# Half of a shift vector's products moved from the gated-delta stage into the gap between output and up projection

## The chip, the cores and the metric

The kernel runs on one core of a Trainium2 chip. The metric is the device time of one execution in microseconds (us); lower is better. TensorE's instructions stand as PE (matmul) and PEld (weight load), VectorE as DVE, ScalarE as ACT, GpSimd as POOL; SP is the queue from which nearly all transfers are issued, in order.

## The reference, cut to what matters

One layer with adaptive modulation, on 128 context and 256 latent tokens of width 2048, all in float32:

```
mod = SiLU(cond) @ w_ada + b_ada          # cond: two vectors; w_ada: 2048 x 12288
shift1, scale1, gate1, shift2, scale2, gate2 = split(mod, 6)
h = RMSNorm(x)*(1+scale1)+shift1
out = mixer(h) @ w_out                    # gated DeltaNet heads and mLSTM heads; w_out 2048 x 2048
x += gate1 * RMSNorm(out)
h = RMSNorm(x)*(1+scale2)+shift2
x += gate2 * RMSNorm(relu(h @ w1)^2 @ w2) # w1 2048 x 8192, w2 8192 x 2048
```

The modulation reads 100 MB of `w_ada` for two rows of result. shift2, scale2 and gate2 (sections 3, 4 and 5 of `mod`, 2048 columns each) are not needed before the second norm, so the kernel computes them beside other work.

## The kernel before

A large product is split: each weight chunk of 2x128 rows (`raw`, 512 KB) is cast to a high part `whi` by ACT and a low part `wlo` by DVE (`wchunk`), and each product is three matmuls (high with low, high with high, low with high). `raw` has three buffers, `whi` and `wlo` two each. `gemm` goes over 8 such chunks for 512 columns of result; with `room`, the last chunks are held in buffers of their own and multiplied row group by row group at the end, so that the first row group is finished early.

The stages that matter here, in order: the last quarters of the gated-delta scan, a chain of small products, with the products of the gate projection between (`ag_block` 0 and 1: `ps_g` from `h`); the transposes of the mixer's output into `yT` (`ps_yT`); the output projection, four `gemm` calls of 512 columns (`mid`), whose weights are `w_out`; then a gap in which DVE adds the residual `x1` (`x<-x,r1r,xr`), the norm factors r1 and r2 of each of the three token tiles are computed (DVE `r1v`, `r20v` to `r22v`, POOL `r1r`, `r20r` to `r22r`), and TensorE transposes the normed tokens (`ps_hT`, with a diagonal matrix `diag` of the factors for the first four of 16 columns of tiles); then the up and down projections of `ffn`.

Modulation work is a list of generators, `S.todo`. `ada_steps` does half a section, 1024 columns, on TensorE: 8 steps of two loads of 512 KB (`raw_ada`) and 8 products of 128x32 with 256 columns, four beside each other in the array (line 206). `ada_vec` does a quarter, 512 columns, on DVE: 8 loads of 512 KB (`raw_av`) and 32 multiply-adds into `adav` (lines 234 and 236). `raw_ada` and `raw_av` share the two buffers of tag `rawa`. After each chunk of a `gemm`, `fill` adds `S.rate` to a credit and runs that many steps; `drain` runs the list down to a given number. A scheduler then orders the instructions of each engine by its own estimates, so that the rows of an engine are not those of the program, but within an engine they run strictly in that order.

In the output projection the chunks are taken as 4, 5, 6, 7, 0, 1, 2, 3; the fourth call holds the last four. The buffers of `yT` for chunks 4 to 7 have the tags `h00` and `h01`, those for chunks 0 to 3 `h10` and `h11`; the activations `hT` of the up projection take these tags over.

Of the kernel before, what the change touches and what calls it, by code (L numbers as in the profile page):

```python
# [12 lines left out]
F32 = mybir.dt.float32  # L13
# [8 lines left out]
P = 128  # L22
D = 2048
NK = D // P
# [10 lines left out]
R1, R2, R3, ND2 = 1.3, 0.9, 0.3, 1  # L35
# [8 lines left out]

def setup(S):
    nc, tc, A = S.nc, S.tc, S.A
    cp, tp = S.cp, S.tp
    c = S.c = SimpleNamespace()

# [167 lines left out]
        ada_mod(S, sec, c0 // P, m, s)  # L217


def ada_vec(S, sec, c0):  # L220

    nc, c = S.nc, S.c
    while S.av is None:
        yield 1
    acc = S.av.tile([P, 2, 512], F32, tag="adav", name="adav", bufs=1)
    for kt in range(NK):
        if kt % 2 == 0:
            raw = S.wp.tile([P, 2, 512], F32, tag="rawa", name="raw_av", bufs=2)
            nc.sync.dma_start(raw, S.A.w_ada[0, kt * P:(kt + 2) * P, sec * D + c0:sec * D + c0 + 512]
                              .rearrange("(k p) n -> p k n", p=P))  # L230
        for v in range(2):
            w = c.scz[:, kt, v:v + 1]
            if kt == 0:
                nc.vector.tensor_scalar(acc[:, v, :], raw[:, 0, :], w, None, op0=ALU.mult)
            else:
                nc.vector.scalar_tensor_tensor(acc[:, v, :], in0=raw[:, kt % 2, :], scalar=w, in1=acc[:, v, :],  # L236
                                               op0=ALU.mult, op1=ALU.add)
        if kt % 2:
            yield 1
    ps = S.pa.tile([P, 512], F32, tag="a", name="ps_av")  # L240
    for j in range(4):
        nc.tensor.matmul(ps[32 * j:32 * j + 32, 0:256], lhsT=c.ones[:, 0:32], rhs=acc[:, j % 2, 256 * (j // 2):][:, 0:256],
                         start=True, stop=True)
    t = ada_cols(S, ps, 256)
    pv = S.wk.tile([P, 4, 2], F32, tag="modsum4", name="modsum4")
    for h in range(2):
        nc.vector.tensor_copy(pv[:, 2 * h:2 * h + 2, :].rearrange("p i v -> p v i"), t[:, 2 * h:2 * h + 2, :, 0])
    ada_mod(S, sec, c0 // P, 4, pv)


def fill(S, n=None):


    S.credit = S.credit + (S.rate if n is None else n) if S.todo else 0.0
    while S.credit >= 1 and S.todo:
        try:
            S.credit -= next(S.todo[0])
        except StopIteration:
            S.todo.pop(0)
            S.credit -= 1  # L260


def drain(S, left):
    while len(S.todo) > left:
        S.credit = 0.0
        fill(S, 1)
    S.credit = max(S.credit, 0.0)


def ada_later(S, sec, nvec=0):  # L270

    for i in range(2):
        if i < 2 - nvec:
            S.todo.append(ada_steps(S, [(sec, 1024 * i + 256 * u) for u in range(4)], 256))
        else:
            S.todo.extend(ada_vec(S, sec, 1024 * i + 512 * h) for h in range(2))
# [52 lines left out]
def alloc_act(S):  # L329

    hh = [[S.hp.tile([P, 8, TOK], F32R, tag=f"h{a}{b}", name=f"h{a}{b}") for b in range(2)] for a in range(2)]
    return lambda kt: (hh[kt // 8][0][:, kt % 8, :], hh[kt // 8][1][:, kt % 8, :])
# [759 lines left out]
def mid(S):  # L1092

    nc, tc, A, c = S.nc, S.tc, S.A, S.c
    S.x1 = [S.fp.tile([P, D], F32, name=f"x1_{t}") for t in range(NT)]
    mp = S.fp
    drain(S, 9 + ND2)
    gp1 = [mp.tile([P, D], F32, tag=("ah", "al")[v], name=f"gp1_{v}", bufs=2) for v in range(2)]
    xr = [mp.tile([P, D], F32, tag=f"y2_{t}", name=f"xr{t}") for t in range(NT)]
    ss = mp.tile([P, NT, 4], F32, name="ssm")  # L1100

    def evac(s, ps, n):
        cs = slice(n * 512, n * 512 + 512)
        junk = mp.tile([P, 512], F32, tag="fj", name="midj", bufs=2)
        nc.scalar.activation(junk, ps, AF.Square, accum_out=ss[:, s, n:n + 1])
        nc.vector.tensor_tensor(S.x1[s][:, cs], ps, gp1[min(s, 1)][:, cs], op=ALU.mult)

    def load(n, i):

        if i in (4, 5):  # L1110
            cs = slice(n * 512, n * 512 + 512)
            nc.sync.dma_start(gp1[i - 4][:, cs], S.gpd[0][i - 4][cs].partition_broadcast(P))
        if n > 0 and i == 6:
            t = n - 1
            nc.sync.dma_start(xr[t], A.x_prompt[0] if t == 0 else A.x_sample[0, (t - 1) * P:t * P])

    kps = [4, 5, 6, 7, 0, 1, 2, 3]
    for n in range(4):
        if n == 3:
            drain(S, 5)  # L1120
            S.rate = 0.0
        room = ()
        if n == 3:
            t = [mp.tile([P, 2, 2, 512], F32R, tag=t, name=f"w_{t}", bufs=2) for t in ("ah", "al")]
            room = [None, None] + [[x[:, i] for i in range(2)] for x in t]
        gemm(S, False, wcols(A.w_out[0], n * 512), kps, S.yT, lambda s, ps, n=n: evac(s, ps, n),
             between=lambda i: load(n, i), room=room)
    S.hT = alloc_act(S)
    ss2 = mp.tile([P, NT, 2], F32, name="ss2")
    diag, r2 = [], []  # L1130
    for t in range(NT):
        s1 = S.wk.tile([P, 1], F32, tag="s1", name="s1")
        nc.vector.tensor_reduce(s1, ss[:, t, :], op=ALU.add, axis=AX.X)
        r = rstd_of(S, s1, 1, 1.0 / D, "r1")
        x1 = S.x1[t]
        for k in range(2):
            cs = slice(k * 1024, (k + 1) * 1024)
            nc.vector.scalar_tensor_tensor(x1[:, cs], in0=x1[:, cs], scalar=r, in1=xr[t][:, cs],
                                           op0=ALU.mult, op1=ALU.add)
            nc.scalar.activation(xr[t][:, cs], x1[:, cs], AF.Square, accum_out=ss2[:, t, k:k + 1])  # L1140
    for t in range(NT):
        s2 = S.wk.tile([P, 1], F32, tag="s1", name="s2")
        nc.vector.tensor_reduce(s2, ss2[:, t, :], op=ALU.add, axis=AX.X)
        r2.append(rstd_of(S, s2, 1, 1.0 / D, f"r2{t}"))
        diag.append(diag_of(S, r2[t], t))
    for kt in range(4):
        build_hT(S, S.x1, kt, 1, diag)
    for t in range(NT):
        nc.scalar.activation(xr[t][:, 512:D], S.x1[t][:, 512:D], AF.Copy, scale=r2[t])
    for kt in range(4, NK):  # L1150
        build_hT(S, xr, kt, 1)


def ffn(S):
    nc, tc, A, c = S.nc, S.tc, S.A, S.c
# [44 lines left out]
                 range(4), act[ch], lambda s, ps, n=n: evac(s, ps, n), psum_dn, room=room)  # L1200

    S.rate = 0.0
    up(0)
    S.rate = R3
    for ch in range(NC):
# [26 lines left out]
def body(tc, A, O):  # L1232
    with ExitStack() as ctx:
        nc = tc.nc
        S = SimpleNamespace(nc=nc, tc=tc, A=A, O=O, todo=[], credit=0.0, rate=1.7, nraw=3, av=None, turn=0)
        ent = ctx.enter_context
        sub = lambda st, nm, bufs=1: st.enter_context(tc.tile_pool(name=nm, bufs=bufs, reuse_waits="tile"))
        S.cp = ent(tc.tile_pool(name="cp", bufs=1))
# [11 lines left out]
        with ExitStack() as mx:  # L1250
# [20 lines left out]
            delta_static(S)  # L1271
            ada_later(S, 2)
            S.todo.append(gate_step(S, 0))
            ada_later(S, 3)
            ada_later(S, 4, ND2)
            ada_later(S, 5, 2)
            S.todo.append(gate_step(S, 1))
# [41 lines left out]
```

## Time and profile before

| | before |
|---|---|
| median of three runs | 1984.19 us (1980.9 to 1991.94) |
| profiled execution, its own time | 1985.06 us |
| its span | 1983.4 us |
| PE busy | 1921.7 us, 97% of the span |
| DVE busy | 1162.8 us, 59% |
| ACT busy | 711.4 us, 36% |
| loads and stores | 337.25 MB, mean 170 GB/s |

The profile is that of one execution; its span runs from the first to the last recorded instruction, and the time around it is 1.7 us. A plain float32 matmul stands in the trace as two records, a matmul of split operands as one. A matmul's recorded duration is longer than the distance to the next one, since matmuls are pipelined: distances between starts tell what one costs.

### The profile page before, as it was taken

Reading aid. Unit: us, or ns where it says so; the run is one execution under the profiler, and the core shown is the slowest. Engines: PE = TensorE matmul, PEld = TensorE weight load, DVE = VectorE, ACT = ScalarE, POOL = GpSimd, SP = SyncE. Lnnn points to the kernel's source line nnn. Section 1 sums busy time; section 2 is a strip of 40 time slices with the busy share of each in tenths; the row PEclk is TensorE's granted clock in tenths of the full one; section 3 lists DMA queues with packets and bytes.
Section 4 is the critical chain, followed back from the end, with each engine's and each line's share of the span. In section 5 each row is a group of like instructions: output and inputs, shape, how many; then the busy total and the mean of one; then the engine's idle time right before and its main releaser. Section 6 shows DMA issues by size and latency. Waiting matters only on the chain.

```text
span 1983.4 us, 28842 instructions
## 1 busy us (share of the span) xinstructions
PE 1921.7 (97%) x11334; PEld 1672.1 (84%) x11334; DVE 1162.8 (59%) x2146; ACT 711.4 (36%) x1125; POOL 129.6 (7%) x138
## 2 busy tenths in 40 slices
PE   5999999999999999998999999999999999999998
PEld 4777888888888777877998998998989989989886
DVE  3767886778777847889633245638343443343445
ACT  4222244634445324335333342332332423323322
POOL 3000000100000000000100010000000100000002
PEclk8999999999999999999999999999999999999999
DMA  9987447575656558764544444645444444444453
GB/s 282 308 294 232 117 131 223 163 222 159 199 161 195 161 166 272 254 213 125 182 127 128 128 127 151 188 128 182 133 124 127 126 131 126 129 131 126 130 172 127
DMA packets 229909, 337.25 MB, mean 170 GB/s; under 512 B 43809, under 2 KB 113137, under 8 KB 228749
## 3 DMA queue, kind: packets, MB, share of 16 engines
q1 hardware_dynamic: 211640, 333.14, 53.8%
q10 hardware_dynamic: 17620, 2.11, 0.7%
q8 instruction: 89, 1.46, 0.3%
q0 software_dynamic: 512, 0.15, 0.1%
q14 instruction: 48, 0.39, 0.1%
HBM read 326.80 MB, written 8.56 MB: 169 GB/s over the span
## 4 chain that ended last, share of the span: by engine, by line
PE 82%; DVE 7%; DMA 6%; issue 1%; POOL 1%; ACT 1%; SPq 0%; DVEq 0%; POOLq 0%; ACTq 0%
PE ps_g L371 12%; PE ps_g L373 12%; PE ps_g L372 12%; PE ps_dn L375 8%; PE ps_dn L377 8%; PE ps_dn L376 8%; PE ps_g L375 4%; PE ps_g L377 4%; PE ps_g L376 4%; PE ps_ada L206 3%; DMA raw_av<-w_ada 2%; DVE wlo L348 2%; DMA raw_ada<-w_ada 2%; DVE adav L236 1%; DMA dA<-X 1%
## 5 line engine op out<-in xcount | busy, mean ns | idle before, releaser
L348 DVE TENSOR_TENSOR wlo<-raw,whi 128x1024 fp32r<-128x1024 f32 (+1 forms) x402 | 486.3, 1210 | 571.6 <-ACT whi L347 563.4
L347 ACT CAST whi<-raw 128x1024 fp32r<-128x1024 f32 (+1 forms) x402 | 417.3, 1038 | 1005.1 <-PE ps_g L372 434.9
L371 PE MATMUL ps_g<-h,whi 128*128 128x384 f32 x1536 | 522.6, 340 | 0.1
L373 PE MATMUL ps_g<-h,wlo 128*128 128x384 f32 x1536 | 518.4, 338 | 3.7 <-DVE wlo L348 3.7
L372 PE MATMUL ps_g<-h,whi 128*128 128x384 f32 x1536 | 518.5, 338 | 0.1
L371 PEld LDWEIGHTS ps_g<-h,whi 128*128 128x128 f32 x1536 | 290.1, 189 | 12.6 <-issue 7.8
L373 PEld LDWEIGHTS ps_g<-h,wlo 128*128 128x128 f32 x1536 | 290.0, 189 | 7.4 <-DVE wlo L348 6.1
L375 PE MATMUL ps_dn<-whi,al 128*128 128x512 f32 x756 | 294.6, 390 | 0.0
L376 PE MATMUL ps_dn<-whi,ah 128*128 128x512 f32 x756 | 294.5, 390 | 0.0
L377 PE MATMUL ps_dn<-wlo,ah 128*128 128x512 f32 x756 | 294.4, 389 | 0.1
L372 PEld LDWEIGHTS ps_g<-h,whi 128*128 128x128 f32 x1536 | 290.0, 189 | 2.6 <-issue 1.8
L375 PEld LDWEIGHTS ps_dn<-whi,al 128*128 128x128 f32 x756 | 141.9, 188 | 30.7 <-issue 1.2
L377 PEld LDWEIGHTS ps_dn<-wlo,ah 128*128 128x128 f32 x756 | 141.9, 188 | 29.8 <-DVE wlo L348 0.5
L376 PEld LDWEIGHTS ps_dn<-whi,ah 128*128 128x128 f32 x756 | 141.9, 188 | 29.2
L236 DVE SCALAR_TENSOR_TENSOR adav<-raw_av,scz,adav 128x512 f32<-128x512 f32 x180 | 127.8, 750 | 10.7 <-DMA raw_av<-w_ada 10.6
L1173 POOL TENSOR_TENSOR rl<-rl 128x384 f32<-128x384 f32 x64 | 69.7, 1096 | 873.3 <-ACT ah L1172 873.2
L375 PE MATMUL ps_g<-whi,h 128*128 128x512 f32 x288 | 118.0, 410 | 0.0
L376 PE MATMUL ps_g<-whi,h 128*128 128x512 f32 x288 | 114.2, 396 | 0.0
L377 PE MATMUL ps_g<-wlo,h 128*128 128x512 f32 x288 | 113.6, 396 | 0.0
L206 PE MATMUL ps_ada<-raw_ada,scz 128*32 128x256 f32 (+1 forms) x1216 | 82.3, 382 | 11.9 <-DMA raw_ada<-w_ada 11.7
L377 PE MATMUL ps_g<-wlo,y 128*128 128x512 f32 x180 | 71.2, 396 | 2.2 <-DVE wlo L348 2.2
L375 PE MATMUL ps_g<-whi,y 128*128 128x512 f32 x180 | 71.1, 395 | 0.0
(409 smaller groups left out, 1843.3 us busy)
## 6 DMA issues: line engine op xcount, KB each, us to landing
raw<-w_ffn SPq DMA_DIRECT2D x256, 512.0 KB, 3.8
raw_ada<-w_ada SPq DMA_DIRECT2D x80, 512.0 KB, 4.5
raw<-w_in SPq DMA_DIRECT2D x74, 512.0 KB, 4.7
raw_ada<-w_ada SPq DMA_DIRECT2D x128, 256.0 KB, 4.5
raw_av<-w_ada SPq DMA_DIRECT2D x48, 512.0 KB, 4.3
raw<-w_in SPq DMA_DIRECT2D x76, 256.0 KB, 4.1
raw<-w_out SPq DMA_DIRECT2D x32, 512.0 KB, 4.9
x<-x_sample SPq DMA_DIRECT2D x2, 1024.0 KB, 9.6
```

Of the source, the lines that this page charges most:

```text
L206: nc.tensor.matmul(ps[32 * j:32 * j + 32, 0:n], lhsT=c.scz[:, k + kk, :], rhs=raw[:, kk, u * n:u * n + n], start=done[j] == 1, stop=done[j ...
L236: nc.vector.scalar_tensor_tensor(acc[:, v, :], in0=raw[:, kt % 2, :], scalar=w, in1=acc[:, v, :], op0=ALU.mult, op1=ALU.add)
L347: nc.scalar.copy(hi, raw)
L348: nc.vector.tensor_tensor(lo, raw, hi.bitcast(F32), op=ALU.subtract)
L371: nc.tensor.matmul(o, lhsT=hi[:, kk, w], rhs=al, start=st, stop=False)
L372: nc.tensor.matmul(o, lhsT=hi[:, kk, w], rhs=ah, start=False, stop=False)
L373: nc.tensor.matmul(o, lhsT=lo[:, kk, w], rhs=ah, start=False, stop=sp)
L375: nc.tensor.matmul(o, lhsT=al[:, w], rhs=hi[:, kk, :], start=st, stop=False)
L376: nc.tensor.matmul(o, lhsT=ah[:, w], rhs=hi[:, kk, :], start=False, stop=False)
L377: nc.tensor.matmul(o, lhsT=ah[:, w], rhs=lo[:, kk, :], start=False, stop=sp)
L1173: nc.gpsimd.tensor_tensor(rl, rl, rl, op=ALU.mult)
```

## The change

The second half of shift2 (section 3, columns 1024 to 2047) leaves the list. Its 16 row blocks of 512 KB are loaded one by one and multiplied in one run of 64 products between the output projection and the up projection (`ada_gap`). Seven of the loads are issued during the third and fourth `gemm` of the output projection, into free parts of the slots of `gp1`, three new tiles and the two `rawa` buffers; six go into `h00` and `h01`, which are free once chunks 4 to 7 of the last `gemm` are multiplied; three more follow in the `rawa` buffers. `S.keep` holds the five items of gate2 back until the up projection, where before some of them ran in the output projection.

```diff
+def ada_gap(S, sec, c0, homes):
+    nc, c = S.nc, S.c
+    raws = []
+    def load():
+        k = len(raws)
+        raws.append(homes[k] if k < len(homes) and homes[k] is not None else
+                    S.wp.tile([P, 1024], F32, tag="rawa", name="raw_gap", bufs=2))
+        nc.sync.dma_start(raws[k], S.A.w_ada[0, k * P:(k + 1) * P, sec * D + c0:sec * D + c0 + 1024])
+    def products():
+        while len(raws) < len(homes):
+            load()
+        ps = S.pa.tile([P, 512], F32, tag="a", name="ps_gap")
+        for k in range(NK):
+            if k == len(raws):
+                load()
+            for u in range(4):
+                nc.tensor.matmul(ps[32 * u:32 * u + 32, 0:256], lhsT=c.scz[:, k, :],
+                                 rhs=raws[k][:, 256 * u:256 * u + 256], start=k == 0, stop=k == NK - 1)
+        ada_mod(S, sec, c0 // P, 8, ada_cols(S, ps, 256).rearrange("p j i v -> p (j i) v"))
+    return load, products
...
-    S.credit = S.credit + (S.rate if n is None else n) if S.todo else 0.0
-    while S.credit >= 1 and S.todo:
+    S.credit = S.credit + (S.rate if n is None else n) if len(S.todo) > S.keep else 0.0
+    while S.credit >= 1 and len(S.todo) > S.keep:
...
 def mid(S):
-    drain(S, 9 + ND2)
-    gp1 = [mp.tile([P, D], F32, tag=("ah", "al")[v], name=f"gp1_{v}", bufs=2) for v in range(2)]
+    drain(S, 8 + ND2)
+    S.keep = 5
+    slots = [mp.tile([P, 3072], F32, tag=("ah", "al")[v], name=f"gp1_{v}", bufs=2) for v in range(2)]
+    gp1 = [t[:, 0:D] for t in slots]
+    homes = [t[:, D:3072] for t in slots] + [mp.tile([P, 1024], F32, name=f"gap{i}") for i in range(3)] + [None, None]
+    gap_load, gap_products = ada_gap(S, 3, 1024, homes)
...
+        if n == 2 and i % 2 or n == 3 and i in (1, 3, 5):
+            gap_load()
...
+    for i in range(2):
+        t = S.hp.tile([P, 3072], F32, tag=f"h0{i}", name=f"hgap{i}")
+        homes += [t[:, 1024 * j:1024 * j + 1024] for j in range(3)]
+    gap_products()
     S.hT = alloc_act(S)
...
     S.rate = 0.0
+    S.keep = 0
     up(0)
...
-            ada_later(S, 3)
+            ada_later(S, 3, 0, 1)
```

Three places of the engines' orders show what moves. The first is TensorE at the end of the last delta quarter: `ps_o` is the last product of the scan, `ps_g` from `h` the gate projection, `ps_yT` a transpose of the mixer's output. Before, gate products were left after the scan and steps of `ps_ada` stood among them and among the transposes:

```order
L1052 MATMUL ps_o_7693<-vv_7634,at_6826 128x128
L375 MATMUL ps_g_7740<-whi_7893,h11_171 128x512
L376 MATMUL ps_g_7740<-whi_7893,h10_170 128x512
L377 MATMUL ps_g_7740<-wlo_7894,h10_170 128x512
L375 MATMUL ps_g_7726<-whi_7917,h11_171 128x512
...
L377 MATMUL ps_g_7740<-wlo_7954,h10_170 128x512
L741 MATMUL ps_yT_7994<-ident_121,yB0_87 128x128
L741 MATMUL ps_yT_7994<-ident_121,yB1_88 128x128
L741 MATMUL ps_yT_7994<-ident_121,yB2_89 128x128
L741 MATMUL ps_yT_8000<-ident_121,yB0_87 128x128
L206 MATMUL ps_ada_7400<-raw_ada_7980,scz_152 32x256 x4
L206 MATMUL ps_ada_7400<-raw_ada_7978,scz_152 32x256 x4
```

Now, at the same place:

```order
L1044 MATMUL ps_z_7651<-r_7647,Tm1_3410 128x128
L1044 MATMUL ps_z_7651<-r_7649,Tm1_3410 128x128
...
L1078 MATMUL ps_o_7682<-S0_7567,qe_6828 128x128
L1078 MATMUL ps_o_7682<-vv_7623,at_6826 128x128
L403 MATMUL ps_g_7729<-wlo_7883,h10_170 128x512
L767 MATMUL ps_yT_7911<-ident_121,yB0_87 128x128
L767 MATMUL ps_yT_7911<-ident_121,yB1_88 128x128
L767 MATMUL ps_yT_7911<-ident_121,yB2_89 128x128
L767 MATMUL ps_yT_7917<-ident_121,yB0_87 128x128
```

All 8 steps of the half (64 products) are gone from the delta stage and from the beginning of the output projection; of the gate projection 39 matmuls stood behind the scan's last product, now one, the others have taken places further ahead.

The second place is TensorE between the output projection (`ps_g` from `y`) and the up projection (`ps_g` from `h`), now (before, the transposes `ps_hT` followed the output projection directly, with the sums `ps_av` of a quarter of gate2 among them):

```order
L403 MATMUL ps_g_8831<-w_al_8810,y10_7909 128x512
L240 MATMUL ps_gap_9027<-gp1_0_8042,scz_152 32x256 x4
...
L240 MATMUL ps_gap_9027<-hgap1_9020,scz_152 32x256 x12
L240 MATMUL ps_gap_9027<-raw_gap_9080,scz_152 32x256 x4
L336 MATMUL ps_hT_9165<-diag_9147,x1_0_8039 128x128
...
L240 MATMUL ps_gap_9027<-raw_gap_9086,scz_152 32x256 x4
L336 MATMUL ps_hT_9174<-diag_9163,x1_2_8041 128x128
...
L240 MATMUL ps_gap_9027<-raw_gap_9092,scz_152 32x256 x4
L338 MATMUL ps_hT_9204<-ident_121,xr2_8049 128x128
L397 MATMUL ps_g_9324<-h01_9107,whi_9320 128x384
```

The products of row blocks 0 to 13 stand ahead of the first transpose; block 14 stands within the transposes and block 15 just ahead of the first matmul of the up projection.

The third place is the SP queue from the last loads of the output projection on. Before:

```order
L343 DMA raw<-w_out 128x2x512
L229 DMA raw_av<-w_ada 128x2x512
L343 DMA raw<-w_ffn 128x2x512 x3
L229 DMA raw_av<-w_ada 128x2x512 x2
L343 DMA raw<-w_ffn 128x2x512 x2
```

Now:

```order
L369 DMA raw<-w_out 128x2x512 x9
L230 DMA hgap_9020<-w_ada 128x1024
L230 DMA hgap_9019<-w_ada 128x1024 x3
L230 DMA hgap_9020<-w_ada 128x1024 x2
L369 DMA raw<-w_ffn 128x2x512 x5
L230 DMA raw_gap<-w_ada 128x1024 x3
```

Six loads stand ahead of the first five of the up projection's weights, and the last three behind them.

## Rows read from the trace of the kernel before

**Rows 1.** The page: busy time of the engines, and transfers.

```profile
PE 1921.7 (97%) x11334; PEld 1672.1 (84%) x11334; DVE 1162.8 (59%) x2146; ACT 711.4 (36%) x1125; POOL 129.6 (7%) x138
...
DMA packets 229909, 337.25 MB, mean 170 GB/s; under 512 B 43809, under 2 KB 113137, under 8 KB 228749
```

**Rows 2.** Busy time by stage: length, then PE, PEld, DVE, ACT, POOL, PEclk, DMA share, GB/s.

```profile
675.00:763.00 88.00, 84.48 (x701) 65.62 (x700) 55.56 (x143) 36.11 (x80) 2.86 (x2) 1.00 0.55 167
763.00:891.60 128.60, 126.36 (x561) 100.88 (x560) 105.13 (x152) 41.26 (x59) 1.53 (x2) 1.00 0.76 254
891.60:907.20 15.60, 6.78 (x39) 4.67 (x38) 12.85 (x29) 10.99 (x16) 2.98 (x4) 0.78 0.43 135
1270.00:1940.00 670.00, 670.00 (x3387) 606.43 (x3386) 290.15 (x310) 212.06 (x253) 48.46 (x43) 1.00 0.45 135
```

**Rows 3.** Timeline of PE from output to up projection: start, us, operation.

```profile
891.23 0.39 PE L377 MATMUL ps_g<-w_al,y 128*128 128x512 f32 x1
899.85 1.65 PE L310 MATMUL ps_hT<-diag,x 128*128 128x128 f32 x6 [8.22 <-DVE s L1143]
...
905.60 0.94 PE L310 MATMUL ps_hT<-diag,x 128*128 128x128 f32 x6
...
907.16 0.44 PE L371 MATMUL ps_g<-h,whi 128*128 128x384 f32 x1
```

**Rows 4.** The operations of line 206 between 675 and 763 us.

```profile
L206 PE MATMUL ps_ada<-raw_ada,scz x128: 379/379/404, 675.9 to 762.2; 128*32 128x256 f32 x128
```

**Rows 5.** Timeline of PE around one such step.

```profile
740.30 0.39 PE L377 MATMUL ps_g<-wlo,h 128*128 128x512 f32 x1
740.62 1.07 PE L206 MATMUL ps_ada<-raw_ada,scz 128*32 128x256 f32 x16
...
741.96 0.40 PE L376 MATMUL ps_g<-whi,h 128*128 128x512 f32 x1
```

**Rows 6.** Timeline of PE in the fourth call of the output projection.

```profile
874.92 0.39 PE L375 MATMUL ps_g<-whi,y 128*128 128x512 f32 x1
875.15 0.39 PE L376 MATMUL ps_g<-whi,y 128*128 128x512 f32 x1
```

**Rows 7.** Timeline of the SP queue.

```profile
875.26 5.07 SPq L343 DMA_DIRECT2D raw<-w_ffn  x3
...
891.01 1.50 SPq L343 DMA_DIRECT2D raw<-w_ffn  x2
```

**Rows 8.** Two stretches as in rows 2, and landing times of `raw`, 860 to 915 us.

```profile
760.00:780.00 20.00, 20.00 (x100) 15.38 (x99) 11.41 (x18) 5.26 (x6) 0.00 (x0) 1.00 0.91 299
DMA to landing us min/median/max: 3.8/4.2/6.1
```

**Rows 9.** Timeline of DVE in the gap.

```profile
889.77 2.35 DVE L348 TENSOR_TENSOR wlo<-raw,whi 128x1024 fp32r<-128x1024 f32 x2
...
895.16 0.74 DVE L236 SCALAR_TENSOR_TENSOR adav<-raw_av,scz,adav 128x512 f32<-128x512 f32 x1
895.82 0.15 DVE L297 TENSOR_SCALAR r1v<-s 128x1 f32<-128x1 f32 x1
...
903.39 0.29 DVE L325 TENSOR_SCALAR diag<-ident,r22r 128x128 f32<-128x128 f32 x1 [0.65 <-POOL r22r L299]
```

**Rows 10.** Waits of PE (675 to 763, then 907 to 1940), and timeline around one `ps_av`.

```profile
PE ps_w L942 <- DMA Nx<-dA: 1.9, 1, 1.9
...
PE ps_g L373 <- DVE wlo L348: 1.8, 4, 0.7
...
1223.10 0.39 PE L377 MATMUL ps_dn<-wlo,ah 128*128 128x512 f32 x1
...
1224.32 0.39 PE L376 MATMUL ps_dn<-whi,ah 128*128 128x512 f32 x1
```

**Rows 11.** Two stretches of the gap, columns as in rows 2.

```profile
900.00:902.00 2.00, 2.00 (x8) 1.38 (x8) 1.57 (x6) 1.60 (x5) 0.98 (x1) 0.50 0.00 0
904.00:906.00 2.00, 2.00 (x19) 1.47 (x19) 1.63 (x4) 1.23 (x3) 0.00 (x0) 1.00 0.72 244
```

More of the change, by code (lines that the diff above doesn't have):

```diff
@@ L267, in drain, with ada_later @@
     S.credit = max(S.credit, 0.0)
-def ada_later(S, sec, nvec=0):
-    for i in range(2):
+def ada_later(S, sec, nvec=0, halves=2):
+    for i in range(halves):
         if i < 2 - nvec:
@@ L1234, in body @@
         nc = tc.nc
-        S = SimpleNamespace(nc=nc, tc=tc, A=A, O=O, todo=[], credit=0.0, rate=1.7, nraw=3, av=None, turn=0)
+        S = SimpleNamespace(nc=nc, tc=tc, A=A, O=O, todo=[], credit=0.0, rate=1.7, nraw=3, av=None, turn=0, keep=0)
         ent = ctx.enter_context
```

## The prediction

> **What bounds the kernel now.** I read the page first: PE is busy 97% of the span [rows 1], so work taken off PE, or time in which PE waits, is what counts. Then I asked where the rest of the span goes, by stages [rows 2]. From 675 to 763 us, the end of the delta scan with the transposes, PE is idle 88.0 - 84.48 = 3.5 us; in the output projection 2.2 us; over 670 us of the up and down projections nothing. The gap from 891.6 to 907.2 us has 8.8 us of idle PE in 15.6. The timeline shows its form [rows 3]: the last product of the output projection starts at 891.23, the first transpose at 899.85, and the trace counts 8.22 us of waiting, for DVE's norm chain. From 899.85 to the first up product at 907.16 PE does transposes and waits in pieces. So the kernel is bound by PE nearly everywhere but there, and the change puts PE work there.
>
> **What the work costs where it stands now.** Between 675 and 763 us line 206 has 128 records [rows 4]; a float32 matmul leaves two, so these are the 64 products, 8 steps. For the cost of a step I take distances of starts [rows 5]: the matmul before it starts at 740.30, the second one behind it at 741.96, 1.66 us. Undisturbed matmuls here follow at 0.227 us (875.15 - 874.92 is 0.23 [rows 6]), so two distances are 0.45, and the step costs 1.66 - 0.45 = 1.21 us, the change of array shape included. 8 x 1.21 = 9.7 us leave a stretch in which PE is 96% busy.
>
> Not all of it need come back as time. The scan is a chain, and the steps were also filler in it. The order after the change has other filler, gate products drawn forward, but then only one is left behind the last `ps_o`, where 39 stood. The transposes that follow have to wait for the copies by ACT and DVE with less beside them. Bounds: nothing returns (idle stays at 3.5 us), or only the three steps behind the scan (two at 740 to 747, one at 761) are gained, 3.6 us. I take 1.0 us of new idle at the transposes, so -8.7: the order shows that filler is there.
>
> **What it costs in the gap.** 64 products are 16 row blocks; a step of two blocks is busy 1.07 us [rows 5], its end beside what follows, so a block takes about 0.50 us and blocks 0 to 12 6.5 us from 891.5: they end at 898.0, inside the wait. What decides is when the loads land.
>
> - The six loads into `h00` and `h01` wait for the last product of chunk 7. Behind it stand 72 matmuls (three row groups, four chunks, six each) at 0.227, 16.3 us, ending at 891.5: they can go at 875.1 [rows 3, 6]. Before, SP issued the first three `w_ffn` loads from 875.26 to 880.3, and the next two at 891.0, when the first casts had freed buffers [rows 7].
> - A busy stretch moves 299 GB/s at 0.91 of the DMA engines [rows 8]; so 0.524 MB take 1.75 us. Six loads: 10.5 us plus some 1.5 to begin, 887.1. `w_ffn` 1, 2 and 3 behind them: 888.9, 890.6, 892.4.
> - The casts of chunks 1 and 2 stand ahead of the residual's last pieces on DVE; `wlo` took 889.77 to 892.1 [rows 9]. Now the second is cast at 891.9 and ready at 893.1, 1.0 us later. Queued behind it on DVE are the second half of token tile 1, the evacuation of tile 2 and with it the whole norm chain, for which PE's transposes wait. Against this the sums `adav` are gone from the gap: 0.66 us of distance for the one ahead of `r1v` (895.16 to 895.82) [rows 9], and one each ahead of `r21v` and `r22v`. Net, I work out `r1v` at 895.2 for 895.8, the diagonal of tile 2 at 901.7 for 903.4.
> - `w_ffn` 4 and 5 go when `wlo` 1 and 2 are done, 891.9 and 893.1; the `raw_gap` loads of blocks 13 and 14 then go at 893.8 and 894.5. Landing takes 3.8 to 6.1 us, median 4.2 [rows 8]: 898.5 and 899.8 with the queue. Block 13 is multiplied at 899.0, just when the first transpose becomes possible. Block 15 needs the buffer of block 13: issued at 899.1, landed at 902.9 to 905.2. It stands just ahead of the first up product, which needs the first `h`, some 3 us after the last diagonal: 904.5 to 905.5.
>
> So the first up product comes at about 905.5 instead of 907.16: -1.7 us. Bounds: -2.7 (block 15 at its earliest, chain at 904.5) to +1.5, when block 15 takes the longest landing plus one more load ahead of it. The shift of columns 8 to 15 is ready near 906 to 908; PE has four chunks of the first eight columns ahead of that, 96 products at about 0.175, 17 us, so this wait is covered; without cover it would cost about 2 us. What bends first if loads are late is the product of block 13, in front of all transposes.
>
> **What moves into the projections.** Of gate2's four quarters about one ran by the gap, and now all four run in `ffn`. One adds a `ps_av` and its transposes: from 1223.10 to the second product behind it, 1224.32, less two distances, is 0.77 us [rows 10], with the transposes 1.0. Its 32 multiply-adds on DVE (busy 43% of 1270 to 1940 [rows 2]) delay `wlo` now and then: PE waited 1.8 us for it there, over three quarters [rows 10], 0.6 each. So +1.5 (0.8 to 2.5). gate2 itself is needed in the last chunk only and is not late. In the output projection the loads are about as many as before (7 in place of some 8 `raw_av`), so I count nothing; the cover is the third call's slack, and a late `w_out` chunk would cost up to its landing, 4 us.
>
> **The sum.** -9.7 + 1.0 - 1.7 + 1.5 = -8.9 us. The profiled execution took 1985.06 us, so 1976.2 by its own time; it lies 0.9 above the median of 1984.19, and against that the forecast is 1975.3, 0.45% faster. About 0.5%, 9.9 us, is what a measurement of this kernel can tell from no change.
>
> **The rivals.**
>
> *More is gained.* If the 39 gate products fit into the scan's waits, so that `ps_o` ends when it did, PE gains these 39 x 0.227 = 8.8 us and the three steps behind, 12.4 in place of 8.7: 1971.6. For it: PE waited 1.9 us at once for a transfer there [rows 10], within the 3.5 idle. Against: 3.5 us of idle cannot hold 8.8 less the five steps that leave, 6.1, and new waits too. Also PE's clock: in the gap the granted clock was 0.50 in 900 to 902, 1.2 GHz, after 8 us without work, and 1.00, 2.4 GHz, from 904 to 906 [rows 11]; six transposes took 1.65 us there and 0.94 later [rows 3]. With products in the wait the clock may stay full, which is worth up to 2 us over 18 such records if nothing else is waited for, and the sum 1973.3. The Trainium skill ("TensorE: Matmul & The Clock Gate", Part 1) has an idle array fall to half its clock until activity releases it; the trace agrees with 0.50, and by that rule the change would gain more than I counted, to 1973.3.
>
> *The stage before is bound by its chain.* Then only the steps behind the scan count: -3.6 - 1.7 + 1.5 = -3.8, 1980.4. For it: waits on transfers and on POOL in the scan; against: PE at 96%.
>
> *Slower: the last loads.* From 875.1 to the landing of block 15 fourteen loads go through one queue, 7.3 MB. All the up projection stands behind block 15 on PE, and the gain outside the gap is 9.7 - 1.0 - 1.5 = 7.2, so the change loses from a first up product at 914.4 on. At the span's mean of 170 GB/s [rows 1] the fourteen take 43 us and land at 918; the first up product follows near 919, +11.8 - 7.2 = +4.6: 1988.8. By 0.5% it loses from 924. For it: `w_ffn` loads, two of them waiting for casts, stand ahead of the three. Against: 299 GB/s where loads are ready to go [rows 8]. [...]
>
> *Nothing is moved* is excluded: the order shows it.
>
> **How the numbers follow.** Forecast 0.47 (its own range 1972 to 1979), more gained 0.24 (filler 0.14, clock 0.10), chain-bound 0.18, slower 0.10, 0.01 left. The range 1968.5 to 1985 takes in the first three cases with their bounds and leaves out half of the slower one and the ends. Faster by over 0.5% is below 1974.3: all of "more" and about 0.17 of the forecast, 0.41; slower by over 0.5% is above 1994.1: part of the slower case and what I have not thought of, 0.08; the rest, 0.51, is within.
>
> **What would show it.** In the changed profile: the output projection ends some 8 to 9 us sooner after the scan's start; PE shows `ps_gap` for about 8 us where 8.2 us of wait stood, with under 2 us of wait for `raw_gap` and the granted clock near 1.00; the first up product comes 14 us (before 15.9) after the last output product; the last `raw_gap` lands before the first `h`. Wrong would be: PE waiting more than 3 us on `ps_gap`, idle in the stage of the transposes above 5 us, or more than 2 us of new waits for `wlo` in the first up projection.

## The result and the profile after

The changed kernel takes 1977.72 us (median of 12 runs, 1973.54 to 1985.01), the kernel before 1986.88 us (median of 12, 1980.9 to 1991.94). The ratio is 0.995, with a 95% interval of 0.9937 to 0.9964: 0.5% faster, some 9.9 us (7 to 13 by the interval; 9.2 by the two medians), and the interval leaves out 1. The forecast was 0.45% (8.9 us) and 1975.3 us. The profiled execution of the changed kernel has a span of 1975.3 us, 8.1 less than before. Its page shows the same work on every engine as [rows 1]:

```profile
PE 1921.8 (97%) x11334; PEld 1675.1 (85%) x11334; DVE 1164.0 (59%) x2146; ACT 711.7 (36%) x1125; POOL 129.9 (7%) x138
```

The stages, cut at about the same work as in [rows 2] (length; PE, PEld, DVE, ACT, POOL; PEclk, which is the granted clock as a share of 2.4 GHz, DMA share, GB/s):

```profile
675.00:753.40 78.40, 74.63 (x571) 61.81 (x571) 55.47 (x147) 34.71 (x78) 3.76 (x2) 1.00 0.30 86
753.40:881.70 128.30, 127.83 (x567) 102.41 (x565) 89.29 (x123) 43.51 (x60) 1.10 (x2) 1.00 0.80 274
881.70:898.30 16.60, 14.01 (x156) 9.12 (x156) 11.19 (x26) 9.72 (x15) 2.11 (x4) 0.79 0.60 191
1261.00:1931.00 670.00, 670.00 (x3388) 606.71 (x3387) 289.32 (x309) 211.29 (x250) 48.46 (x43) 1.00 0.46 137
```

The first stage is 9.6 us shorter. The gap has 14.01 us of busy PE in place of 6.78, and it is longer, not shorter.

**A common mark.** TensorE's order of instructions is the same before and after for its first 3548 instructions, up to a `ps_ks` product in the last delta quarter. The time up to there I do not count as the change's: the SP queue parts some 14 us earlier, but the two kernels stood 1.1 us apart before that already. TensorE's timeline of the kernel before shows this product at

```profile
675.58 0.38 PE L1009 MATMUL ps_ks<-Sn,slq 128*128 128x128 f32 x2
```

and that of the changed kernel at

```profile
676.66 0.38 PE L1035 MATMUL ps_ks<-Sn,slq 128*128 128x128 f32 x2
```

In the 14 profiled executions of this study it starts anywhere from 671.1 to 681.5, so a difference of two spans holds several microseconds of chance. I therefore count three pieces from the mark: to the start of the last output product, from there to the start of the first up product (the gap), and from there to the end.

| kernel | mark to last output product | gap | PEclk in it | rest | from the mark | ratio to the kernel before (95%) |
|---|---|---|---|---|---|---|
| before | 215.65 | 15.93 | 0.79 | 1076.2 | 1307.8 | 1 |
| changed | 204.75 | 16.91 | 0.80 | 1077.0 | 1298.6 | 0.9950 (0.9937 to 0.9964) |
| changed, again (e9) | 204.75 | 14.92 | 0.89 | 1077.8 | 1297.5 | 0.9946 (0.9923 to 0.9968) |
| half left out (e1) | 211.77 | 15.23 | 0.67 | 1074.1 | 1301.1 | 0.9951 (0.9938 to 0.9965) |
| 16 homes (e2) | 207.68 | 14.62 | 1.00 | 1075.7 | 1298.0 | 0.9941 (0.9928 to 0.9953) |
| by token tile (e3) | 206.00 | 15.51 | 0.89 | 1076.8 | 1298.3 | 0.9946 (0.9932 to 0.9960) |
| both (e4) | 206.49 | 16.25 | 0.94 | 1076.5 | 1299.3 | 0.9959 (0.9946 to 0.9972) |
| before, filled (e5) | 214.89 | 15.25 | 1.00 | 1075.5 | 1305.6 | 0.9974 (0.9961 to 0.9987) |
| changed, filled (e6) | 206.12 | 13.98 | 1.00 | 1077.0 | 1297.1 | 0.9944 (0.9928 to 0.9961) |
| held back alone (e7) | 215.80 | 17.75 | 0.62 | 1075.4 | 1308.9 | 1.0003 (0.9991 to 1.0015) |
| moved alone (e8) | 207.15 | 16.90 | 0.80 | 1083.1 | 1307.1 | 0.9963 (0.9945 to 0.9982) |
| blocks 5, 6 first (e10) | 206.09 | 13.46 | 1.00 | 1077.3 | 1296.8 | 0.9926 (0.9908 to 0.9944) |
| e10 by token tile (e11) | 206.02 | 13.35 | 1.00 | 1077.5 | 1296.8 | 0.9924 (0.9905 to 0.9943) |
| e10 not held back (e12) | 206.27 | 14.72 | 0.88 | 1081.6 | 1302.6 | 0.9951 (0.9933 to 0.9970) |

Each execution ran once with a profile; the ratios are from the timed runs. Kernels with the same order of instructions in a piece still differ in it: the first piece of the changed kernel's order is 204.75 to 206.12 in six executions (changed, e9, e3, e6, e10, e11), and of before's order 214.89 to 215.80 in three.

**The gap after.** TensorE's timeline, to be read against [rows 3]:

```profile
881.41 0.39 PE L403 MATMUL ps_g<-w_al,y 128*128 128x512 f32 x1
...
884.77 2.77 PE L240 MATMUL ps_gap<-hgap,scz 128*32 128x256 f32 x48
889.56 0.64 PE L240 MATMUL ps_gap<-raw_gap,scz 128*32 128x256 f32 x8 [2.02 <-DMA raw_gap<-w_ada]
890.13 0.74 PE L336 MATMUL ps_hT<-diag,x 128*128 128x128 f32 x4
891.45 1.65 PE L336 MATMUL ps_hT<-diag,x 128*128 128x128 f32 x6 [0.57 <-DVE diag L351]
893.02 1.08 PE L240 MATMUL ps_gap<-raw_gap,scz 128*32 128x256 f32 x8
894.04 3.36 PE L336 MATMUL ps_hT<-diag,x 128*128 128x128 f32 x14
...
897.66 0.64 PE L240 MATMUL ps_gap<-raw_gap,scz 128*32 128x256 f32 x8
...
898.32 0.42 PE L397 MATMUL ps_g<-h,whi 128*128 128x384 f32 x1
```

The products of blocks 0 to 12 run without a wait, then TensorE stands 2.0 us for block 13's load, and the transposes behind it are slow: six records in 1.65 us, as in the kernel before after its long wait. The granted clock (third column from the end) shows why:

```profile
888.00:890.00 2.00, 0.44 (x8) 0.16 (x8) 1.11 (x5) 2.00 (x6) 0.54 (x1) 1.00 0.60 242
890.00:892.00 2.00, 1.43 (x10) 1.07 (x7) 0.59 (x3) 2.00 (x3) 0.54 (x1) 0.67 0.41 49
892.00:894.00 2.00, 2.00 (x14) 1.00 (x12) 0.86 (x2) 1.53 (x2) 0.00 (x0) 0.50 0.56 217
896.00:898.00 2.00, 2.00 (x17) 1.58 (x16) 1.85 (x5) 0.28 (x1) 0.00 (x0) 0.62 0.57 214
898.00:900.00 2.00, 2.00 (x20) 1.74 (x13) 0.65 (x4) 0.79 (x2) 0.00 (x0) 1.00 0.27 38
```

From 890 to 898 us TensorE runs mostly at 1.2 GHz. DVE, by contrast, is early. Its timeline, for [rows 9]:

```profile
880.81 2.35 DVE L374 TENSOR_TENSOR wlo<-raw,whi 128x1024 fp32r<-128x1024 f32 x2
...
885.06 0.15 DVE L323 TENSOR_SCALAR r1v<-s 128x1 f32<-128x1 f32 x1
...
891.11 0.29 DVE L351 TENSOR_SCALAR diag<-ident,r22r 128x128 f32<-128x128 f32 x1 [0.65 <-POOL r22r L325]
```

The last diagonal comes 9.7 us after the start of the last output product (891.11 - 881.41; before 903.39 - 891.23 = 12.2). But from it to the first up product 7.2 us pass, where before it was 3.8. The SP queue, for [rows 7]:

```profile
864.85 3.01 SPq L230 DMA_DIRECT2D hgap<-w_ada  x6
867.95 15.61 SPq L369 DMA_DIRECT2D raw<-w_ffn  x5
884.58 6.01 SPq L230 DMA_DIRECT2D raw_gap<-w_ada  x3
```

The last three loads go from 884.58 on, when the products of blocks 5 and 6 have freed the two shared buffers.

### The profile page after: what moved, and what is told of

The parts are those of the page before. It is cut to its first block, busy times and chain, and to the rows that moved or that the text cites. A ratio compares the mean times of both kernels' runs of the same rounds, so it can differ in the third digit from the quotient of the medians.

```text
span 1975.3 us, 28843 instructions
## 1 busy us (share of the span) xinstructions
PE 1921.8 (97%) x11334; PEld 1675.1 (85%) x11334; DVE 1164.0 (59%) x2146; ACT 711.7 (36%) x1125; POOL 129.9 (7%) x138
## 4 chain that ended last, share of the span: by engine, by line
PE 85%; DVE 6%; DMA 6%; ACT 1%; issue 1%; POOL 1%; SPq 0%; DVEq 0%; ACTq 0%; POOLq 0%
PE ps_g L397 12%; PE ps_g L399 12%; PE ps_g L398 12%; PE ps_dn L401 9%; PE ps_dn L403 9%; PE ps_dn L402 9%; PE ps_g L401 4%; PE ps_g L402 4%; PE ps_g L403 4%; PE ps_ada L206 3%; DVE wlo L374 1%; DMA dA<-X 1%; DVE adav L262 1%; DMA raw_av<-w_ada 1%; PE ps_num L730 1%
## 5 line engine op out<-in xcount | busy, mean ns | idle before, releaser
L397 PEld LDWEIGHTS ps_g<-h,whi 128*128 128x128 f32 x1536 | 290.1, 189 | 12.2 <-issue 7.6
L206 PE MATMUL ps_ada<-raw_ada,scz 128*32 128x256 f32 (+1 forms) x1088 | 74.4, 386 | 9.9 <-DMA raw_ada<-w_ada 8.5
```

The source lines that it names most:

```text
L206: nc.tensor.matmul(ps[32 * j:32 * j + 32, 0:n], lhsT=c.scz[:, k + kk, :], rhs=raw[:, kk, u * n:u * n + n], start=done[j] == 1, stop=done[j ...
L397: nc.tensor.matmul(o, lhsT=hi[:, kk, w], rhs=al, start=st, stop=False)
```

## The experiments

My theory after the result (B in the expectations) was that the gap did not get shorter because of the clock: the wait for block 13 lets it fall, and the transposes pay. Rivals: the late loads by themselves (A), TensorE's in-order queue standing behind blocks 13, 14 and 15; and the order of the transposes (C), of which 20 of 24 records now stand behind the last diagonal. Before the change 16 did: 10, then sums, then 6 more. The expectation of e1 counts the 10 alone, so that this rival had less to explain than it says. The first four runs try the three theories, e5 and e6 the clock by itself, e7 and e8 split the change into its two parts, and e9 to e12 try a remedy.

**e1: the half left out.**

```diff
     def products():
-        while len(raws) < len(homes):
-            load()
+        return ada_mod(S, sec, c0 // P, 8, c.scz[:, 0:8, 0:2])
...
-            gap_load()
+            pass
```

> The changed kernel without the 16 loads and the 64 products of the half (columns 1024 to 2047 of shift2 are taken from a resident tile instead, so that half of the shift is not computed). It shows how long the gap is when nothing is put into it. The gap is counted from the start of the last output product to the start of the first up product: 15.9 us before the change, 16.9 after it. Theory A, late loads (TensorE's in-order queue stands behind the loads of blocks 13 to 15): the gap is 13.5 to 14 us, that is 3 us less than with the half, because DVE's norm chain is 2.3 us shorter than before. Theory B, the clock (granted clock 0.50 in the transposes, whatever stands ahead of them): the gap is 16 us or more, since TensorE then has no work for 8 us. Theory C, the order of the transposes (20 records behind the last diagonal in place of 10): 15.5 to 16 us. Total against the kernel before: -10 to -13 us (ratio 0.994 to 0.995) by A, -9 by C, -8 by B.

It did not measure what it was meant to. With no `raw_gap` loads in the two shared buffers the scheduler drew gate2's sums forward again: between the first and the last load of `w_out` 23 loads `raw_av` are issued, 14 in the changed kernel, 21 before. The sums stand in the gap too, and TensorE's transposes begin after a wait of 5.27 us at half clock:

```profile
894.98 1.65 PE L335 MATMUL ps_hT<-diag,x 128*128 128x128 f32 x6 [5.27 <-DVE s L1178]
```

In the output projection DVE is late, as the waits of TensorE from 753 to 888 us show (total, times, longest):

```profile
PE ps_g L402 <- DVE wlo L373: 3.8, 3, 2.7
```

So the gap's length with nothing in it stays open. What follows is another thing: to leave the half out altogether (0.9951) is no faster than to move it (0.995). The moved loads also hold the sums' buffers, and with them there DVE has fewer sums to do in the output projection.

**e2: a home for each of the 16 blocks.**

```diff
...
-        if n == 2 and i % 2 or n == 3 and i in (1, 3, 5):
+        if n == 1 and i == 7 or n == 2 and i % 2 or n == 3 and 0 < i < 6:
...
+            homes.append(S.av.tile([P, 2, 512], F32, tag="adav", name="gapx", bufs=1).rearrange("p a b -> p (a b)"))
+            g3 = mp.tile([P, 768], F32, name="gap3")
+            rl = [mp.tile([P, TOK], F32, tag="rl", name="gaprl", bufs=3) for _ in range(3)]
+            hf = [S.wk.tile([P, TOK], F32, tag="hfull", name="gaphf") for _ in range(2)]
+            homes.append([g3[:, 0:256], g3[:, 256:512], g3[:, 512:768], rl[0][:, 0:256]])
+            homes.append([rl[1][:, 0:256], rl[2][:, 0:256], hf[0][:, 0:256], hf[1][:, 0:256]])
```

> The changed kernel with a buffer of its own for each of the 16 row blocks (three more homes, the last two in pieces of 256 columns), so that no load of the half stands behind the loads of the up projection's weights and all 64 products can run in one piece. Theory A, late loads: no wait for a load ahead of the first transpose or among the transposes, gap 14 to 15 us in place of 16.9, total 2 to 3 us below the changed kernel, 11 to 12 below the kernel before (ratio 0.9943). Theory B, the clock: the light products of 32 columns, or the wait behind them, let the granted clock fall to 0.50 all the same; gap 16 to 17 us, ratio 0.995 to 0.996. Theory C, the order of the transposes: 16 us, ratio 0.9955.

The 64 products run in one piece, the granted clock is 1.00 over the whole gap, and the gap is 14.62 us, as the first reading had it. But with the wait for block 13 gone the clock stayed up too, so the run does not part late loads from the clock; that the clock falls whatever stands ahead of the transposes did not happen in this execution. TensorE now waits for DVE:

```profile
894.45 1.38 PE L342 MATMUL ps_hT<-diag,x 128*128 128x128 f32 x10 [1.11 <-DVE diag L357]
```

The two shared buffers came free so early that sums stand on DVE ahead of the copies `hfull`, which the first up product needs:

```profile
894.71 2.07 DVE L268 SCALAR_TENSOR_TENSOR adav<-raw_av,scz,adav 128x512 f32<-128x512 f32 x3
```

Part of the gain is lost ahead of the gap (207.68 in place of 204.75 to 206.12). Two more loads stand in the output projection there; that they are the cause is not shown.

**e3: the transposes token tile by token tile.**

```diff
-    for kt in range(4):
-        build_hT(S, S.x1, kt, 1, diag)
+    pss = [S.pm.tile([P, 512], F32, tag="m", name="ps_hT") for kt in range(3)]
+    for t in range(NT):
+        for kt in range(3):
+            nc.tensor.matmul(pss[kt][:, t * P:(t + 1) * P], lhsT=S.x1[t][:, kt * P:(kt + 1) * P], rhs=diag[t], start=True, stop=True)
...
```

> The changed kernel with the first nine transposes written token tile by token tile, so that those of token tiles 0 and 1 stand ahead of those that need the last diagonal; the loads stand as in the changed kernel. Theory C, the order: the 20 records behind the last diagonal become about 10 to 12, gap 1 to 2 us shorter than 16.9, ratio 0.9945. Theory A, late loads: the transposes gain little, because block 14's and block 15's products stand among them and wait for their loads: gap 16.5 to 17, ratio unchanged at 0.995. Theory B, the clock: they run at 0.50 in either order, gap 16 to 16.5.

The gap is 15.51 us, between the two executions of the changed kernel (16.91 and 14.92). Whether the order is worth anything this run alone cannot say; e11 can.

**e4: both edits.**

> Both edits: a buffer of its own for each row block, and the transposes token tile by token tile. If late loads and order are separate causes, the gap is 13 to 14 us (3 to 4 below the changed kernel) and the total 12 to 13 us below the kernel before, ratio 0.9935 to 0.994. If only the clock counts, the gap stays at 15.5 to 16.5 us and the ratio at 0.995. If one of the two is all, the gap is that of the run with this edit alone.

The gap is 16.25 us, in the range of the second reading (15.5 to 16.5), though the clock was at 0.94 in the mean. It is longer than with either edit alone, so the two did not add up. The transposes wait longer for `hfull`, behind the same sums, and the clock falls late:

```profile
897.67 1.62 PE L344 MATMUL ps_hT<-diag,x 128*128 128x128 f32 x6 [1.52 <-DVE hfull L349]
```

**e5 and e6: dense products where TensorE waits.** In the kernel before 33, in the changed kernel 10 ahead of block 13; their result is unused.

```diff
+                for q in range(10):
+                    nc.tensor.matmul(pd, lhsT=FW[:, 0, 0, 0:P], rhs=FW[:, 0, 0, :], start=q == 0, stop=q == 9)
```

> The kernel before, with 33 dense products (128x128 with 128x512, resident operands, result unused) added between output projection and transposes, where TensorE waits for 8.22 us. They add work and compute nothing. Theory B, the clock: the granted clock stays at 1.00 through the transposes, where it was 0.50 to 0.78; the gap falls from 15.9 to 14.5 to 15.3 us, and the total by about 1 us (ratio 0.9992 to 1.0000). If the chain of DVE alone sets the gap, it stays at 15.9 us at any clock, ratio 1.000. If the fill outlasts the wait, the gap grows by up to 1 us.

The clock stays at 1.00 and the gap is 15.25 us, 0.7 less, as the first reading had it: the last diagonal comes 12.1 us after the last output product (12.2 before), so DVE's chain sets most of it. In the timed runs the kernel is 0.26% faster, 5 us, more than expected, with 2.6 as the lower end of the interval; by the pieces of one execution it is 2.2. Where the rest comes from I can't show.

> The changed kernel, with ten such dense products (result unused) ahead of the product of row block 13, so that TensorE works where it waits 2.0 us for that block's load. They add work and compute nothing. Theory B, the clock falls because of this wait: granted clock 1.00 in the transposes, gap 14.5 to 15.5 us in place of 16.9, ratio 0.994 to 0.9945. Theory A, late loads alone: TensorE stands for blocks 14 and 15 instead, gap 16.5 to 17 us, ratio 0.995.

The gap is 13.98 us at a clock of 1.00, although the fill adds 2.5 us of work. All 24 records of the first transposes now take 2.94 us, where 14 took 3.36:

```profile
890.65 2.57 PE L242 MATMUL ps_fill<-w_al 128*128 128x512 f32 x10
...
894.70 2.94 PE L340 MATMUL ps_hT<-diag,x 128*128 128x128 f32 x24
```

TensorE waits only 0.34 us for block 14. The gap is 0.9 to 2.9 us shorter than in the two executions of the changed kernel. The loads of blocks 13 and 14 went out as there, 3.2 us after the last output product, but the scheduler had also put block 14's product ahead of all transposes, where it stood among them, so this run alone does not part clock and order. One order at two clocks does: the changed kernel and its repetition e9, and e10 and e12 below. They show that the clock is worth 1.3 to 2 us of the gap. That the wait is what lets it fall is likely from e6, one execution, and not more than that: in e12 it fell with no wait above 1.11 us. The timed runs do not show a gain (0.9944).

**e7 and e8: each part of the change alone.** In e7 `S.keep = 5` is put into the kernel before; in e8 it is taken out of the changed kernel:

```diff
     drain(S, 8 + ND2)
-    S.keep = 5
```

> The kernel before with gate2's five items held back to the up projection, and the half of shift2 left where it was. If holding them back is what shortened DVE's chain in the gap (2.3 us), the gap is 13.6 to 14.5 us and the total 1 to 2 us below the kernel before (ratio 0.999 to 0.9995). If it is instead that the moved loads hold the two buffers of the sums, the sums are drawn back into the gap all the same, and gap and total stay as before: 15.9 us, ratio 1.000.

Holding back alone does nothing (1.0003): sums are drawn into the gap all the same. Its gap of 17.75 us was not expected. On TensorE and on DVE it has the same instructions in the same order as before (15.93); the granted clock is 0.62 in place of 0.79, and the 10 records that took 1.38 us take 2.50.

> The changed kernel with gate2's items not held back; the half is moved. If holding them back is of weight, sums of gate2 take DVE time in the output projection and the gap: gap 18 to 19 us, ratio 0.996. If the moved loads hold the sums' buffers anyway, all is as in the changed kernel: gap 16.5 to 17.5 us, ratio 0.995.

The gap is the changed kernel's, as the second reading has it. What I had not expected is the rest, 1083.1 us, 6 more; e12 takes that up. One wait in it shows the clock again, far from the gap:

```profile
1187.24 0.47 PE L401 MATMUL ps_dn<-whi,al 128*128 128x512 f32 x1 [2.04 <-DVE y L1222]
```

From 1188 to 1191 us the granted clock is 0.50, and the products there follow at 0.43 us in place of 0.23.

**e9 to e12: a remedy.** e9 is the changed kernel again. I expected its gap at 16.5 to 17.3 us, and it is 14.92. Its transposes stand behind the same wait (2.09 us), but the clock is back at 1.00 from 894 us on, and the 14 records that took 3.36 us take 1.83:

```profile
893.67 0.69 PE L240 MATMUL ps_gap<-raw_gap,scz 128*32 128x256 f32 x8
894.29 1.83 PE L336 MATMUL ps_hT<-diag,x 128*128 128x128 f32 x14
```

> The changed kernel itself, for a comparison on one chip with the next three. Gap 16.5 to 17.3 us with the granted clock at 0.50 in the transposes, ratio 0.994 to 0.996.

In e10 the blocks of the shared buffers are multiplied first, e11 adds the order of e3, and e12 is e10 without `S.keep = 5`:

```diff
-        for k in range(NK):
+        for k in [5, 6] + [k for k in range(NK) if k not in (5, 6)]:
...
-                                 rhs=raws[k][:, 256 * u:256 * u + 256], start=k == 0, stop=k == NK - 1)
+                                 rhs=raws[k][:, 256 * u:256 * u + 256], start=k == 5, stop=k == NK - 1)
```

> The changed kernel with the two row blocks of the shared buffers (5 and 6) multiplied first instead of after blocks 0 to 4, so that their buffers come free 2.2 us sooner and the loads of blocks 13 and 14 can go sooner. Nothing is added. Late loads as the cause that lets the clock fall: the wait of 2.0 us for block 13 shrinks to under 0.5, the granted clock stays at 1.00, the 24 records of the first transposes take 2.9 us, gap 14 to 14.8 us, ratio 2 to 3 us (0.0010 to 0.0015) below that of the changed kernel. If the loads are late because the loads of the up projection's weights stand ahead of them and not because of the buffers, the wait stays at 1.5 to 2 us and gap and ratio are the changed kernel's.

The SP queue of e10 issues the loads of blocks 13 and 14 (`raw_gap` x2) at

```profile
872.26 14.42 SPq L369 DMA_DIRECT2D raw<-w_ffn  x4
886.77 0.89 SPq L230 DMA_DIRECT2D raw_gap<-w_ada  x2
887.77 0.38 SPq L369 DMA_DIRECT2D raw<-w_ffn  x1
```

1.1 us after the last output product (885.66), in the changed kernel 3.2. Two things moved them. The buffers came free sooner, and the scheduler also put the two loads ahead of the fifth load of the weights, which in the changed kernel stands in front of them and was issued by 2.15 us (867.95 + 15.61 - 881.41). From there they waited another 1.0 us for the buffers. So of the 2.1 us about half can be put down to the buffers and the rest to the place in the queue; no run here changes one without the other. TensorE:

```profile
891.61 0.61 PE L240 MATMUL ps_gap<-raw_gap,scz 128*32 128x256 f32 x8
892.71 0.64 PE L240 MATMUL ps_gap<-raw_gap,scz 128*32 128x256 f32 x8 [0.48 <-DMA raw_gap<-w_ada]
...
895.71 2.50 PE L336 MATMUL ps_hT<-diag,x 128*128 128x128 f32 x20 [1.11 <-DVE diag L351]
```

and the gap in one row (length, PE, PEclk, DMA share, GB/s):

```profile
885.66:899.12 13.46, 11.52 (x157) 1.00 0.67 235
```

The gap is 13.46 us, and the kernel is the fastest in its group but for e11: 1975.72 us (median), against 1978.99 for e9 and 1989.09 for the kernel before on that chip. The 3.3 us to e9 are inside the two intervals, so only the gap can be called better. For it there are three executions with this order of products (13.46, 13.35 in e11 and 14.72 in e12) against two of the changed kernel (16.91 and 14.92).

> The same with the first nine transposes token tile by token tile. With the clock at 1.00 the order is worth less than the 1.4 us it gave at half clock: gap 13 to 13.8 us (0.5 to 1 below the run before), ratio 0.993 to 0.994, the fastest so far. If the order counts as much as before: gap 12.6 to 13.2 us. If transposes wait for DVE's copies as in the run with 16 homes and both edits: gap 15 to 16 us.

13.35 us and 0.9924: at full clock the order of the transposes is worth 0.1 us, by one execution of each. That is the answer to the third theory.

> Blocks 5 and 6 first, and gate2's items not held back. In the run with the move alone the gap was as in the changed kernel, and the stretch from the first up product to the end took 1083.1 us in place of 1077.0, with waits for DVE of 5.1 us in place of 2.2. If holding back counts there, it is 1080 to 1084 again and the ratio 0.0015 to 0.003 above that of the run with blocks 5 and 6 first. If that was chance of one execution, both stand within 0.001 of each other.

The rest is 1081.6 us, 4.3 above e10, and the ratio is 0.0025 above e10's, as expected, though the two intervals overlap a little. Without holding back, the sums stand beside the down projections: 32, 32 and 24 of DVE's operations into `adav` fall into the first three of them, in e10 6, 11 and 17, with the others beside the up projections. In the first down projection DVE is busy 54.65 us of 1000 to 1100, 34.76 in e10, and TensorE waits for `wlo`; in the second and third, at 1192, 1209 and 1329 us, it waits for DVE's additions into `y`. Waits from 900 us on:

```profile
PE ps_dn L401 <- DVE y L1222: 3.0, 3, 1.4
PE ps_dn L403 <- DVE wlo L374: 1.9, 4, 0.8
```

In e10 there are no waits for `y`, and 2.1 us for `wlo`, so waits make 3.0 of the 4.3 us. The gap of e12 has another lesson. Up to the 20 transposes it has the instructions and, within 0.03 us, the waits of e10, but they take 3.87 us:

```profile
896.16 3.87 PE L336 MATMUL ps_hT<-diag,x 128*128 128x128 f32 x20 [1.11 <-DVE diag L351]
```

The granted clock was 0.50 from 896 to 898 us there and 1.00 in e10.

## Why the prediction came out as it did

**The work that leaves the delta stage** was forecast at -9.7, with +1.0 of new idle at the transposes. From the mark to the last output product the order before takes 215.4 us (mean of three executions) and the order after 205.6 (mean of six): -9.8. In the two profiled kernels alone it is 215.65 - 204.75 = 10.9, of which TensorE's busy time is 9.4 (209.90 to 200.51) and idle 1.5. So 1.21 us for a step, taken from [rows 5], held; that idle would grow by 1.0 did not. New waits came at the place named, as the waits of TensorE from 735 to 760 us show (before 0.4 us in all):

```profile
PE ps_yT L767 <- DVE y L770: 1.2, 2, 0.6
PE ps_yT L767 <- ACT ojunk L1083: 0.8, 1, 0.8
```

But in these two profiles they were more than made up in the output projection, where I had counted nothing. There the waits for `wlo` went from 2.2 us to

```profile
PE ps_g L403 <- DVE wlo L374: 0.3, 1, 0.3
```

DVE does 60 multiply-adds of sums there and did 85 before (42.0 and 59.7 us), since the moved loads hold their buffers. In the other executions of this order the wait is 0.5 to 1.8 us, which is why I keep to the mean.

**The gap** was forecast 1.7 us shorter. By the single profiles it is 1.0 longer; with a second execution of each order (16.91 and 14.92 against 15.93 and 17.75) it is 0.9 shorter, with 2 us of scatter, so its sign is not settled. Counted from the last output product, block 13 was forecast at 7.8 us and came at 8.2, `r1v` at 4.0 and came at 3.7, the last diagonal at 10.5 and came at 9.7. These steps held. The one that failed is that the first up product needs "the first `h`, some 3 us after the last diagonal", with the granted clock near 1.00: it took 7.2 and 5.2 us. The forecast allowed up to 3.8 (905.5 - 901.7), the distance of the kernel before (907.16 - 903.39), where 16 records stood behind the last diagonal, the 6 of [rows 3] at 905.60 and

```profile
903.73 1.38 PE L310 MATMUL ps_hT<-diag,x 128*128 128x128 f32 x10 [0.52 <-DVE diag L325]
```

and the clock was back. Now 20 stood there, and the clock fell behind the wait for block 13 (0.67 in 890 to 892, 0.50 in 892 to 894), which at 2.0 us was at the edge of what I had allowed (under 2 us). With the clock at 1.00 the distance is 3.75 us (e10, 899.12 - 895.37) with the same 20 records. I had the rule for this among my rivals, as a gain. The Trainium skill ("TensorE: Matmul & The Clock Gate", Part 1) has activity release the clock's throttle; the one execution of e6, with its fill and its 1.00, agrees. My mistake was to count the products as cover for the whole wait and not to ask what the clock does in the part that they leave.

**The projections**, forecast +1.5: the rest is 1077.2 us in the mean of the same six executions and 1076.2 before, +1.0; against the 1075.4 of e5 it would be +1.8. What I gave no weight is that this term hangs on `S.keep`: without it the rest is 4 to 6 us longer (e8, e12) and the timed gain 0.37% in e8, and 0.49% in e12 where e10 has 0.74%.

**The sum** of the means is -9.8, -0.9 (or +1.0 by the single profiles) and +1.0, so -9.7, for 9.9 measured and 8.9 forecast. The total agreed because the new idle was counted too high by about as much as the gap too well; that much of it is luck.

**The rivals.** "More is gained" by filler did not come: the last `ps_o` stands 61.1 us behind the mark (737.78 - 676.66), before 59.9, although five steps less lie between, so the gate products did not all fit into the scan's waits. Its second half, the clock, was right in that the clock moves the gap by up to 2 us, but this kernel did not keep it (0.80, before 0.79); e10 and e11, at 1.00, show gaps 2.5 us shorter than before. "Bound by its chain" had -3.6 for the first term and is excluded by the -9.8. "Slower: the last loads": block 15's product starts at 897.66 without a wait; fourteen loads did not pile up.

## What to carry to other kernels

Work put into a wait was worth its full time where it came from (9.8 us for 9.7), but look at what stands behind it: if a short wait is left at its end, here 2.0 us, TensorE's clock may fall and the next products pay for it. Multiply first what holds the buffers that later loads need, and see where the scheduler then puts those loads. And where a scheduler fills free buffers with whatever comes next, a load that occupies a buffer decides as much about the order as the line that asks for it.

## What the runs showed of the hardware

The clock is not set by the instructions alone. The same order with the same waits (0.46 to 0.48, 0.34 to 0.37 and 1.11 us) ran at 1.00 in e10 and at 0.50 in e12, and after a wait of 2.0 to 2.1 us the clock came back at 898 us in one execution of the changed kernel and at 894 in the other. This makes the gap uncertain by 1.3 to 2 us from one execution to the next.

In short stretches the loads moved faster than I took them. I had 299 GB/s over 20 us from [rows 8]; in the gap a stretch of 2 us reaches 402 GB/s in e10:

```profile
890.00:892.00 2.00, 2.00 (x44) 1.00 1.00 402
```

And a stretch of 3548 instructions on TensorE in one and the same order ended between 671.1 and 681.5 us in the 14 profiles, so that a common mark has to be subtracted before a change of half a per cent can be read from two of them.
